# Second expert search: weight remainders on GpSimd, two of three gathered rows on VectorE, four dense U tiles behind the search

## The chip, the cores and the metric

The kernel runs on one core of one Trainium2 chip. The metric is the device time of one execution in microseconds (us). The core has a matrix engine (TensorE, PE in the profile; its weight loads are PEld), three elementwise engines (VectorE = DVE, ScalarE = ACT, GpSimd = POOL), and DMA queues that move data between HBM and the on-chip memory (SBUF). GpSimd also issues the indirect DMAs that gather rows by index. PSUM is the memory into which TensorE accumulates.

## The reference

One decoder block on 512 tokens of width 1024: three token mixers (forgetting attention, sliding window, memory attention) with gates, and then a product-key expert layer, which is what the change touches:

```python
def peer_ffn(h, w_q, keys1, keys2, u, v):
    q = (h @ w_q).astype(jnp.float32).reshape(B, S, PEER_HEADS, 2, half)
    s1 = jnp.einsum('bshd,hkd->bshk', q[..., 0, :], keys1)
    s2 = jnp.einsum('bshd,hkd->bshk', q[..., 1, :], keys2)
    v1, i1 = lax.top_k(s1, PEER_TOPK)
    v2, i2 = lax.top_k(s2, PEER_TOPK)
    cand = (v1[..., :, None] + v2[..., None, :]).reshape(B, S, PEER_HEADS, PEER_TOPK * PEER_TOPK)
    sv, si = lax.top_k(cand, PEER_TOPK)
    ...
    experts = e1 * N_KEYS + e2
    gates = jax.nn.softmax(sv, axis=-1)
    ...
        a = jnp.einsum('cd,ced->ce', h_c, u[e_c])
        act = jax.nn.gelu(a, approximate=False) * g_c
        return jnp.einsum('ce,ced->cd', act, v[e_c])
```

There are 8 heads, 128 keys in each half, 16 x 8 = 128 chosen experts for a token, and 16384 experts, each with one row of 1024 in `u` and one in `v`.

## The kernel before

**Tiles.** The tokens are four blocks of 128. Block 0 goes through the mixers first, blocks 1 to 3 together behind it. In the expert layer blocks 0 and 1 gather their rows: for each of the 128 choices one indirect DMA brings the `u` row or the `v` row of all 128 tokens (128 x 1024 floats), and one job multiplies and sums it. That makes 512 jobs in a fixed order (`JOBS`): the `u` rows of block 0, its `v` rows, then the same of block 1. Blocks 2 and 3 (`DENSE`) use no gathers: TensorE multiplies them with all of `u` and `v`, in 128 tiles of 128 experts each.

**A job** is one call of `step`. It first issues gathers, so that four rows (later six) lie ahead, into five row buffers, and then takes the oldest row. A `v` row of block 0 can be added in three ways: before PSUM is free, VectorE adds row times weight to `x1[0]` in SBUF (L890); with `apart`, ScalarE scales the row (L886) and GpSimd adds it to `x1[0]` (L887); otherwise VectorE adds row times weight to the tile `two` in PSUM (L893 for the first, L896 for the others), and `x1` gets `two` at the end of the block.

**Split weights.** For more exact products a weight is split into a rounded upper part `whi` (ScalarE, L119) and the remainder `wlo`. `load` fetches the weight, and first calls `pump`, which adds to the shared `credit[0]`, draws on a list of side work, and sets the credit to zero when that list is empty. `rest` makes the remainder: it adds `share[0]` to a counter, and each time the counter reaches one GpSimd does the subtraction (L129), else VectorE (L131). `mm3` then multiplies three times: upper by upper, lower by upper, upper by lower (L145 to L147). `gemm_tr` does this for one block of 128 output columns, 24 matmuls. The pool holds three `wlo` buffers.

**The stages in question.** The second search finds the experts of blocks 1 to 3. For each head two weight blocks (`w_pq`) go through `gemm_tr`, the result is multiplied with the keys (L754), and VectorE takes the best 16 of 128 for three blocks and two halves (`top16`, L711 to L715), then GpSimd sums the candidate pairs (L722) and VectorE takes the best 16 of 64, one head later. Two heads of scores are made ahead. `search` yields a cost of 1.6 for each top 16 of 128 and of 1.2 for each top 16 of 64, 105.6 in all. The loop around it spends these costs: for every `PER_ROW` of credit one job of block 0 is done, and at 104 / `FIRST_U` units each one dense U tile is computed (`dense_u`: 8 matmuls on unsplit data, then a Gelu on ScalarE, L1029 and L1031). The first 13 U tiles are fetched in this loop too. The first 183 jobs were done before, beside the mixers.

Behind the search comes the cover: `COVER` further dense U tiles on TensorE, while VectorE weighs the scores (`weigh`), derives the expert numbers of blocks 1 to 3 (`choose`, `numbers_of`, L806 to L850), and does jobs of block 0 between these parts. It starts U tile k with `FIRST_U` and ends with `KEPT` = `FIRST_U + COVER` = 32 tiles. `turn_block` then transposes the choices of a block (L1075, copied by ScalarE at L1077), and the spread begins: 64 batches in which VectorE builds one-hot sides (L1088), ScalarE scales them (L1091), TensorE multiplies them (L1103), while 25 further U tiles run, and 0.95 jobs a batch, every fourth of them apart. The last stage runs over all 128 tiles of `v`, with the remaining U tiles and jobs spread over it.

**Order.** Up to the end of the search a planner orders the instructions of each engine by estimated times and by rank; jobs have the lowest rank (`tc.high_priority(-LATER)`). From the cover on the order of TensorE, VectorE and GpSimd is that of the program.

Of the kernel before, what the change touches and what calls it, by code (L numbers as in the profile page):

```python
# [26 lines left out]
DENSE = (2, 3)  # L27
ND = len(DENSE)
TD = 128 * ND
FIRST_U, COVER, DURING, AFTER = 8, 24, 25, 0  # L30
PRE_U = 13
KEPT = FIRST_U + COVER
SPILT = (128 - KEPT) // 3
# [17 lines left out]
UNREAD = 36  # L51
LATER = 400
PACE = {"search": 20.0, "choose": 8.0, "rows": 3.5}
EARLY_ROWS, PER_ROW = 183, 4.6


@with_exitstack
def tile_block(ctx: ExitStack, tc: tile.TileContext, t: dict, out: bass.AP):
# [39 lines left out]
    due, share = [0.0], [0.0]  # L98
# [115 lines left out]
    def factors(sums, nb):  # L214

        ss = small_f(BIG, "rss", 2)[:, :nb]
        V.reduce_sum(ss, sums[:, :nb], axis=AX.X)
        return rsqrt_mean(ss, nb, D)

    def diagonals(r, nb):  # L220
        dg = small.tile([128, BIG, 128], F32, tag="dg", name="dg", bufs=1)
        for b in range(nb):
            A.activation(dg[:, b], ident, AF.Copy, scale=r[:, b:b + 1])
        return dg

    def turn(xs, g, hi, lo, dg=None, tags=("tp", "sc")):

        w = 128 * len(xs)
        for dc in range(KC):
            ps = bank(tags[dc % len(tags)])  # L230
            for b, x in enumerate(xs):
                dst, src = ps[:, b * 128:(b + 1) * 128], x[:, dc * 128:(dc + 1) * 128]
                if dg is None:
                    PE.transpose(dst, src, ident)
                else:
                    PE.matmul(dst, src, dg[:, b], start=True, stop=True)
            A.activation(hi[dc], ps[:, :w], AF.Copy, scale=g[:, dc:dc + 1])
            if lo:
                V.scalar_tensor_tensor(lo[dc], ps[:, :w], g[:, dc:dc + 1], hi[dc].bitcast(F32),
                                       op0=OP.mult, op1=OP.subtract)  # L240
# [614 lines left out]
    known, issued, done, ahead, flying, rpool = [2 * NJ], [0], [0], [AHEAD], {}, []  # L855
    begun_v = set()

    def step(apart=False):

        while issued[0] < min(known[0], done[0] + ahead[0] + 1):  # L860
            n = issued[0]
            issued[0] += 1
            b, tab, j = JOBS[n]
            if ahead[0] > AHEAD and n % (ROWS_IN + MORE) >= ROWS_IN:
                r = wp.tile([128, WSLOT], F32, tag="raw", name="row")[:, :D]
            else:
                r = rpool[0].tile([128, D], F32, tag="row", name="row", bufs=ROWS_IN)
            G.indirect_dma_start(out=r, out_offset=None, in_=t["peer_" + tab],  # L868
                                 in_offset=bass.IndirectOffsetOnAxis(ap=eidx[b][:, j:j + 1], axis=0))
            flying[n] = r  # L870
        n = done[0]
        done[0] += 1
        b, tab, j = JOBS[n]
        r, c = flying.pop(n), slice(j, j + 1)
        if tab == "u" and b and j == 0:
            A.copy(two[0], h2n[b])
        if tab == "u" and apart:
            G.tensor_tensor(r, r, h2n[b], op=OP.mult)
            A.activation(r, r, AF.Copy, accum_out=acts[b][:, c])
        elif tab == "u":  # L880
            scr = big.tile([128, D], BF16, tag="junk", name="scr")
            tc.keep_in_program_order(
                V.scalar_tensor_tensor(scr, r, 1.0, two[0] if b else h2n[b], op0=OP.mult, op1=OP.mult,  # L883
                                       accum_out=acts[b][:, c]))
        elif apart:
            tc.keep_in_program_order(A.activation(r, r, AF.Copy, scale=acts[b][:, c]))  # L886
            G.tensor_tensor(x1[b], x1[b], r, op=OP.add)  # L887
        elif not two:
            tc.keep_in_program_order(
                V.scalar_tensor_tensor(x1[b], r, acts[b][:, c], x1[b], op0=OP.mult, op1=OP.add))  # L890
        elif b not in begun_v:
            begun_v.add(b)
            tc.keep_in_program_order(V.tensor_scalar(two[0], r, acts[b][:, c], None, op0=OP.mult))  # L893
        else:
            tc.keep_in_program_order(
                V.scalar_tensor_tensor(two[0], r, acts[b][:, c], two[0], op0=OP.mult, op1=OP.add))  # L896
        if j == NJ - 1:
            if tab == "u":
                A.activation(acts[b], acts[b], AF.Gelu)
                V.tensor_mul(acts[b], acts[b], gate[b])  # L900
            else:
                V.tensor_add(x1[b], x1[b], two[0])
# [95 lines left out]
    def fetch_u_to(k):  # L998
        while u_next[0] <= min(k, NK - 1):
            fetch_u(u_next[0])  # L1000
            u_next[0] += 1
# [4 lines left out]
    def dense_u(k):  # L1006

        if k >= FIRST_U:
            fetch_u_to(min(max(k, PRE_U) + URING - 1, LAG) if k < LAG else k)
        w = u_raw.pop(k)  # L1010
        if split_u(k):
            if k % 2:
                hi, lo = (gp[0].tile([128, D], F32R, tag=tag, name=tag, bufs=1) for tag in ("uhi", "ulo"))
            else:
                hi, lo = halves_u[0][:, 0], halves_u[0][:, 1]
            A.copy(hi, w)
            yield
            V.tensor_sub(lo, w, hi.bitcast(F32))
            yield
            ps, hi, lo = bank("mm"), *(x.rearrange("p (n w) -> p n w", n=KC) for x in (hi, lo))  # L1020
            for dc in range(KC):
                mm3(ps[:, :TD], (hi[:, dc], lo[:, dc]), [x[dc] for x in h2s], dc == 0, dc == KC - 1)
            A.activation(ga(k), ps[:, :TD], AF.Gelu)
            return
        w = w.rearrange("p (n w) -> p n w", n=KC)
        yield
        ps = bank("mm")
        for dc in range(KC):
            PE.matmul(ps[:, :TD], w[:, dc], h2f[dc], start=dc == 0, stop=dc == KC - 1)  # L1029
            yield  # L1030
        A.activation(ga(k), ps[:, :TD], AF.Gelu)  # L1031
# [2 lines left out]
    h2T = [chunks(x) for x in pair(BIG)]  # L1034
    h2f = chunks(dp.tile([128, KC, TD], F32, tag="h2f", name="h2f", bufs=1))
    halves_u = []
    k_u, share[0] = 0, 0.0
    with tc.tile_pool(name="qb", bufs=2) as qq:
        turn([x1[b] for b in GROUPS[1]], g2, *h2T)
        spent, dg, credit[0] = 0.0, None, 0.0  # L1040
        for cost in search(qq, h2T, f, BIG):
            spent += cost
            if dg is None and spent > 12.0:
                V.tensor_copy(rstd[:, 1:NB], factors(sums, BIG))
                dg = diagonals(rstd[:, 2:NB], ND)
                turn([x1[b] for b in DENSE], g2, h2f, None, dg)
            while u_next[0] < PRE_U and spent > 6.0 * u_next[0]:
                fetch_u_to(u_next[0])
            credit[0] += cost
            while credit[0] >= PER_ROW and NJ <= done[0] < known[0]:  # L1050
                credit[0] -= PER_ROW
                with tc.high_priority(-LATER):
                    step(apart=True)
            if k_u < FIRST_U and spent > 104.0 / FIRST_U * (k_u + 1):
                list(dense_u(k_u))
                k_u += 1
    assert k_u == FIRST_U, (k_u, spent)

    cp = build.enter_context(tc.tile_pool(name="cp", bufs=1))
    ctx.enter_context(tc.manual_schedule(engines={mybir.EngineType.Pool, mybir.EngineType.DVE, mybir.EngineType.PE}))  # L1060
# [295 lines left out]
```

## Time and profile before

| | |
|---|---|
| median of 3 runs | 1589.84 us (lowest 1589.75; one run at 5559.83) |
| profiled execution | 1593.83 us, its span 1592.1 us |
| PE, PEld busy | 1514.5 us (95%), 1374.6 us (86%) |
| DVE, ACT, POOL busy | 1433.5 us (90%), 829.5 us (52%), 779.0 us (49%) |
| moved by DMA | 531.90 MB, mean 334 GB/s |
| VectorE remainders, L131 (128x1024) | 244 from the weight buffers, 304.2 us |
| rows added on GpSimd, L887 | 23, mean 2375 ns |

Times are counted from the start of the span. A row of a group names line, engine, operation, output and inputs, the shape, how often, the busy time with the mean of one, and the idle time of the engine just before it with what ended most of that. The search lies at about 640 to 755 us, the cover at 755 to 852, the spread from there to 1010, and the last stage goes to the end. A number of the form `(x572)` counts instructions.

### The profile page before, as it was taken

The numbers are of one execution on the slowest core, as the hardware profiler recorded it, in microseconds if no ns is written. First come the engines' busy times: TensorE is split into PE (matmuls) and PEld (weight loads), VectorE is DVE, ScalarE is ACT, GpSimd is POOL, SyncE is SP. The second block draws the span as 40 slices with busy tenths as digits, with TensorE's granted clock in tenths as the row PEclk, the third lists the DMA queues.
The fourth block names the chain that finished last, engine by engine and source line by source line (L and its number), as shares of the span: only waits on it lengthen the run. The fifth ranks groups of instructions, "written<-read, shape, count | busy, mean of one in ns | idle before, by whom it ended". The sixth has DMA issues, their size and how long they took to land.

```text
span 1592.1 us, 27209 instructions
## 1 busy us (share of the span) xinstructions
PE 1514.5 (95%) x9458; PEld 1374.6 (86%) x9458; DVE 1433.5 (90%) x2666; ACT 829.5 (52%) x1840; POOL 779.0 (49%) x639
## 2 busy tenths in 40 slices
PE   8999899999999989999995999899999999999998
PEld 7989799997888988999885898788888888888887
DVE  6678477989899999999899999799999999999998
ACT  7778336646345534454215998554454444454443
POOL 1100015768576455467744665455555454555451
PEclk9999999999999999999997999999999999999999
DMA  8677657898899899965897999999999999999995
GB/s 328 222 236 249 242 182 247 316 357 299 314 346 322 273 348 346 382 217 185 290 411 247 380 393 392 344 399 390 409 410 410 409 411 409 395 409 411 410 409 213
DMA packets 178361, 531.90 MB, mean 334 GB/s; under 512 B 17456, under 2 KB 46384, under 8 KB 178224
## 3 DMA queue, kind: packets, MB, share of 16 engines
q0 software_dynamic: 73728, 268.47, 44.8%
q1 hardware_dynamic: 94416, 225.95, 38.9%
q10 hardware_dynamic: 10080, 35.75, 5.6%
q8 instruction: 74, 1.21, 0.3%
q14 instruction: 63, 0.52, 0.1%
HBM read 515.42 MB, written 14.68 MB: 333 GB/s over the span
## 4 chain that ended last, share of the span: by engine, by line
PE 54%; DVE 13%; issue 12%; DMA 11%; POOL 6%; ACT 4%; DVEq 0%; POOLq 0%; SPq 0%; ACTq 0%
PE mm L146 8%; PE mm L1029 8%; PE mm L147 8%; PE mm L145 8%; DMA row<-in_peer_v_dram,eidx 5%; POOL row L868 4%; DMA row<-in_peer_u_dram,eidx 4%; DVE wlo L131 3%; PE sc L1103 3%; DVE two L896 2%; PE sc L146 1%; PE sc L147 1%; PE sc L145 1%; PE tp L145 1%; PE tp L146 1%
## 5 line engine op out<-in xcount | busy, mean ns | idle before, releaser
L868 POOL DMA_INDIRECT row<-in_peer_v_dram,eidx x256 | 320.9, 1254 | 287.1 <-DVE two L896 162.8
L868 POOL DMA_INDIRECT row<-in_peer_u_dram,eidx x256 | 318.2, 1243 | 237.2 <-DVE scr L883 135.0
L131 DVE TENSOR_TENSOR wlo<-raw,whi 128x1024 fp32r<-128x1024 f32 (+1 forms) x244 | 304.2, 1248 | 33.6 <-ACT whi L119 26.5
L896 DVE SCALAR_TENSOR_TENSOR two<-row,acts,two 128x1024 f32<-128x1024 f32 x176 | 226.2, 1285 | 3.4 <-DMA row<-in_peer_v_dram,eidx 1.1
L119 ACT CAST whi<-raw 128x1024 fp32r<-128x1024 f32 x146 | 152.6, 1050 | 100.4 <-PE mm L146 62.4
L883 DVE SCALAR_TENSOR_TENSOR scr<-row,own 128x1024 bf16<-128x1024 f32 x128 | 156.3, 1221 | 22.2 <-DMA row<-in_peer_u_dram,eidx 21.2
L883 DVE SCALAR_TENSOR_TENSOR scr<-row,two 128x1024 bf16<-128x1024 f32 x117 | 142.2, 1216 | 6.0 <-DMA row<-in_peer_u_dram,eidx 5.0
L203 POOL TENSOR_TENSOR rsy<-rsv,mhalf 128x4 f32<-128x4 f32 (+5 forms) x25 | 39.9, 1600 | 184.3 <-DVE rsv L202 130.5
L1156 ACT CAST ah<-ga 128x256 fp32r<-128x256 f32 x116 | 47.1, 407 | 156.3 <-PE tp L146 118.4
L145 PE MATMUL mm<-hhi,whi 128*128 128x384 f32 x320 | 110.1, 344 | 1.2 <-DVE mg L673 0.7
L1158 ACT CAST whi<-raw 128x1024 fp32r<-128x1024 f32 x96 | 100.4, 1048 | 18.2 <-DMA raw<-in_peer_v_dram 12.7
L146 PE MATMUL mm<-hlo,whi 128*128 128x384 f32 x320 | 109.7, 343 | 0.0
L147 PE MATMUL mm<-hhi,wlo 128*128 128x384 f32 x320 | 108.9, 340 | 0.0
L146 PE MATMUL sc<-wlo,ah 128*128 128x512 f32 x256 | 101.4, 396 | 6.3 <-DVE wlo L131 6.3
L145 PE MATMUL mm<-whi,hhi 128*128 128x256 f32 (+1 forms) x360 | 103.7, 290 | 2.9 <-DVE g L604 1.9
L146 PE MATMUL mm<-wlo,hhi 128*128 128x256 f32 (+1 forms) x360 | 102.6, 286 | 1.7 <-DVE wlo L131 1.6
L147 PE MATMUL mm<-whi,hlo 128*128 128x256 f32 (+1 forms) x360 | 101.9, 285 | 0.8 <-DVE hlo L662 0.8
L147 PE MATMUL sc<-whi,al 128*128 128x512 f32 x256 | 101.8, 398 | 0.0
L145 PE MATMUL sc<-whi,ah 128*128 128x512 f32 x256 | 101.3, 396 | 0.2 <-ACT whi L1158 0.2
L145 PE MATMUL tp<-whi,ah 128*128 128x512 f32 x256 | 101.1, 395 | 0.0
L146 PE MATMUL tp<-wlo,ah 128*128 128x512 f32 x256 | 100.8, 394 | 0.0
L147 PE MATMUL tp<-whi,al 128*128 128x512 f32 x256 | 100.7, 393 | 0.0
(322 smaller groups left out, 4544.9 us busy)
## 6 DMA issues: line engine op xcount, KB each, us to landing
raw<-in_peer_v_dram SPq DMA_DIRECT2D x96, 512.0 KB
hhi<-in_uT_dram ACTq DMA_DIRECT2D x68, 512.0 KB
raw<-in_w_tr_dram SPq DMA_DIRECT2D x48, 512.0 KB
raw<-in_w_nat_dram SPq DMA_DIRECT2D x40, 512.0 KB
last<-in_peer_v_dram SPq DMA_DIRECT2D x32, 512.0 KB
hhi<-in_uT_dram SPq DMA_DIRECT2D x26, 512.0 KB
raw<-in_w_o_dram SPq DMA_DIRECT2D x24, 512.0 KB
gd<-st SPq DMA_DIRECT2D x24, 512.0 KB
```

Of the source, the lines that this page charges most:

```text
L119: (cast or A.copy)(hi[:, :n * w], raw[:, :n * w])
L131: V.tensor_sub(lo, raw, hi.bitcast(F32))
L145: PE.matmul(ps, lh, rh, start=first, stop=False)
L146: PE.matmul(ps, lh, rl, start=False, stop=False)
L147: PE.matmul(ps, ll, rh, start=False, stop=last)
L868: G.indirect_dma_start(out=r, out_offset=None, in_=t["peer_" + tab], in_offset=bass.IndirectOffsetOnAxis(ap=eidx[b][:, j:j + 1], axis=0))
L883: V.scalar_tensor_tensor(scr, r, 1.0, two[0] if b else h2n[b], op0=OP.mult, op1=OP.mult, accum_out=acts[b][:, c]))
L896: V.scalar_tensor_tensor(two[0], r, acts[b][:, c], two[0], op0=OP.mult, op1=OP.add))
L1029: PE.matmul(ps[:, :TD], w[:, dc], h2f[dc], start=dc == 0, stop=dc == KC - 1)
L1103: PE.matmul(ps[:, u], o[:, 1, u], o[:, 0, u], start=True, stop=True)
L1156: A.copy(ah, a)
L1158: A.copy(hi, raw)
```

## The change

Three constants and three lines of the second search are changed. While the search runs, `share[0]` is 1.0 in place of 0.0, so that all 16 remainders of the query weights go to GpSimd. A job counts 4.2 in place of 4.6, and it is done apart (ScalarE and GpSimd) only if its number is divisible by three and the cost spent is under 94; the others go to VectorE and `two`. Four U tiles run in the search in place of eight, and 28 in place of 24 in the cover.

```diff
-FIRST_U, COVER, DURING, AFTER = 8, 24, 25, 0
+FIRST_U, COVER, DURING, AFTER = 4, 28, 25, 0
...
-EARLY_ROWS, PER_ROW = 183, 4.6
+EARLY_ROWS, PER_ROW, APART, NO_APART = 183, 4.2, 3, 94.0
...
-    k_u, share[0] = 0, 0.0
+    k_u, share[0] = 0, 1.0
     with tc.tile_pool(name="qb", bufs=2) as qq:
         turn([x1[b] for b in GROUPS[1]], g2, *h2T)
         spent, dg, credit[0] = 0.0, None, 0.0
...
             while credit[0] >= PER_ROW and NJ <= done[0] < known[0]:
                 credit[0] -= PER_ROW
                 with tc.high_priority(-LATER):
-                    step(apart=True)
+                    step(apart=done[0] % APART == 0 and spent < NO_APART)
             if k_u < FIRST_U and spent > 104.0 / FIRST_U * (k_u + 1):
                 list(dense_u(k_u))
                 k_u += 1
     assert k_u == FIRST_U, (k_u, spent)
+    share[0] = 0.0
```

`KEPT`, and with it the split between gates kept on chip and gates sent through HBM, stays at 32, and `LAG` at 57.

## The prediction

> **What bounds the kernel now.** I read the page's span in slices, then a table of busy time over six stretches cut where the work changes: second search, dense U tiles behind it ("cover"), a gap, the ramp of the spread, the spread, the last stage.
>
> ```profile
> 655.00:755.00 100.00, 99.48 (x572) 95.00 (x572) 98.29 (x585) 48.13 (x73) 61.42 (x63) 1.00 0.67 240
> 755.00:835.00 80.00, 79.21 (x369) 69.41 (x367) 74.63 (x110) 14.19 (x30) 50.75 (x42) 1.00 0.92 350
> 835.00:852.00 17.00, 0.26 (x3) 0.02 (x1) 16.65 (x23) 0.83 (x2) 8.63 (x9) 0.59 0.90 321
> 852.00:870.00 18.00, 16.00 (x88) 14.67 (x89) 17.46 (x21) 15.52 (x57) 5.57 (x6) 0.82 0.49 165
> 870.00:1010.00 140.00, 136.93 (x849) 125.08 (x848) 126.63 (x193) 124.23 (x458) 85.18 (x69) 0.99 1.03 376
> 1010.00:1592.00 582.00, 562.54 (x3215) 490.34 (x3213) 558.96 (x660) 268.74 (x394) 282.37 (x209) 0.99 0.99 392
> ```
>
> The columns are the stretch, its length, the busy us of PE, weight load, DVE, ACT and POOL, the granted clock, DMA share and GB/s. In the search PE (99.5 of 100 us) and DVE (98.3) are both full, DMA is not (0.67). In the cover both stay full. From 835 to 852 PE does 0.26 us and DVE 16.65 of 17: DVE alone decides when the spread starts. The spread is full on PE and DMA, the last stage on DMA (0.99), with DVE at 96%.
>
> The chain in order of time and the waits say how the cover ends:
>
> ```profile
> 762.15 72.79 PE mm L1029 x336
> 834.93 0.33 PE tp L1075 x3
> 835.26 18.74 issue
> ```
>
> ```profile
> ACT eT L1077 <- DVE own L850: 14.9, 1, 14.9
> ```
>
> PE has multiplied its last cover tile and turned block 0 by 835.3; then 18.7 us pass in which only DVE works, and ACT's copy of the turned block waits 14.9 us for DVE's last job before the spread.
>
> ```profile
> L1088 DVE TENSOR_TENSOR o<-tp,eT x64: 1212/1215/1222, 852.2 to 997.4; 128x1024 f32<-128x1024 f32 x64
> ```
>
> L1088 is the spread's first work on DVE. So its start, 852.2, is the later of DVE's end (852) and PE's end (835). What the change takes from DVE pays for 17 us, then PE decides.
>
> **How many rows move.** `pump` sets the shared credit to zero at each weight load, as its work list is empty by then. So rows are counted per head: 9.6 units for head 0, 13.2 each for heads 1 to 4, then 43.2 without a load. At 4.6 a row this gives 2, 4 x 2 and 9: 19 rows. At 4.2 it gives 2, 4 x 3 and 10: 24 rows. Of these, numbers 183 to 206, the condition (divisible by 3, cost under 94) holds for seven; 17 go to DVE. The 19 agree with the trace:
>
> ```profile
> L887 POOL TENSOR_TENSOR mg<-mg,row x23: 2353/2367/2420, 676.4 to 895.2; 128x1024 f32<-128x1024 f32 x23
> ```
>
> 19 of the 23 are the search's, 4 stand in the spread. The cover keeps 36 rows, the spread 60, so the last stage gets 209 rows instead of 214.
>
> **DVE, part by part.** Rows by groups and by line in 640 to 755, and one collision from the timeline:
>
> ```profile
> L131 DVE TENSOR_TENSOR wlo<-raw,whi x14: 1197/1224/3709, 639.3 to 726.0; 128x1024 fp32r<-128x1024 f32 x14
> L131 DVE TENSOR_TENSOR wlo<-raw,whi 128x1024 fp32r<-128x1024 f32 x14 | 23.6, 1683 | 0.5 <-ACT whi L119 0.5
> 715.88 2.41 POOL L887 TENSOR_TENSOR mg<-mg,row 128x1024 f32<-128x1024 f32 x1
> 715.68 3.71 DVE L131 TENSOR_TENSOR wlo<-raw,whi 128x1024 fp32r<-128x1024 f32 x1
> L896 DVE SCALAR_TENSOR_TENSOR two<-row,acts,two x176: 1275/1284/1291, 773.3 to 1573.1; 128x1024 f32<-128x1024 f32 x176
> L711 DVE MAX8 best<-cand 128x8 f32<-128x64 f32 x24 | 4.3, 210 | 1.6 <-POOL cand L722 1.6
> ```
>
> Removed: 16 lower parts, 14 of them in this window with 23.6 us and two ahead of it at 1.22: 26.0 us. Undisturbed the 14 would be 17.1 us, so 6.5 us of it are collisions like the one shown, where 1.22 became 3.71 beside a GpSimd addition. Added: 17 rows into PSUM at 1.284, 21.8 us; that group stays within 1275 to 1291 ns over 176 calls although GpSimd adds beside some of them, so I give it no stretch. Gone also: 1.6 us in which DVE waits for the last candidates behind GpSimd's additions.
>
> GpSimd's additions now run on into the cover and disturb DVE there:
>
> ```profile
> L887 POOL TENSOR_TENSOR mg<-mg,row 128x1024 f32<-128x1024 f32 x6 | 14.2, 2365 | 0.1
> L835 DVE TENSOR_TENSOR hot<-hot 128x1024 bf16<-128x1024 bf16 x6 | 6.1, 1013 | 0.0
> L819 DVE TENSOR_TENSOR rj<-rj,p 128x128 f32<-128x128 f32 x3 | 3.7, 1223 | 0.1
> L820 DVE TENSOR_TENSOR rj<-p,rj 128x128 f32<-128x128 f32 x3 | 0.9, 291 | 0.1
> L807 DVE TENSOR_SCALAR p<-sh 128x128 f32<-128x128 uint32 x3 | 3.3, 1113 | 0.1
> L806 DVE TENSOR_SCALAR sh<-pos 128x128 uint32<-128x128 uint32 x3 | 0.7, 220 | 0.0
> L791 DVE TENSOR_TENSOR gate<-ex,gden 128x128 f32<-128x128 f32 x3 | 2.8, 1034 | 0.0
> ```
>
> Against their equals (L820, L806) the excess is 2.8 us for L819, 2.6 for L807 and about 1.8 for each of L791 and L835: 9.0 us. With seven additions instead of 19, and none behind cost 94, it goes. Sum for DVE: -26.0 + 21.8 - 1.6 - 9.0 = **-14.8 us**; it ends the cover at 837.5.
>
> **PE.** Four tiles move; each is 3.45 us, by ACT's Gelu that follows each:
>
> ```profile
> 772.81 0.38 ACT L1031 ACTIVATE ga<-mm 128x256 f32<-128x256 f32 x1 [3.07 <-PE mm L1029]
> 776.26 0.38 ACT L1031 ACTIVATE ga<-mm 128x256 f32<-128x256 f32 x1 [3.07 <-PE mm L1029]
> 655.41 0.34 PE L145 MATMUL mm<-hhi,whi 128*128 128x384 f32 x1
> 659.09 0.34 PE L145 MATMUL mm<-hhi,whi 128*128 128x384 f32 x1
> ```
>
> So 13.8 us leave the search and come back in the cover; nothing vanishes. PE was full in both, hence its end stays at 835 plus whatever it now waits for. The pair of matmuls, seven triples apart, gives 0.526 us a triple, 4.2 us for the 24 matmuls of one weight block. GpSimd must deliver one lower part per block at 2.37 (L887, the same shape) instead of DVE's 1.22. Its load in the window:
>
> ```profile
> L887 POOL TENSOR_TENSOR mg<-mg,row 128x1024 f32<-128x1024 f32 x14 | 33.4, 2384 | 4.9 <-ACT row L886 4.7
> L868 POOL DMA_INDIRECT row<-in_peer_v_dram,eidx x23 | 24.8, 1077 | 12.5 <-DVE rss L217 3.5 <-POOL cand L722 2.9 <-DVE mg L890 1.5
> L722 POOL TENSOR_TENSOR cand<-v 128x48 f32<-128x48 f32 (+2 forms) x32 | 13.0, 418 | 28.1 <-DVE v L714 18.4 <-DVE v L711 8.9 <-DMA raw<-in_w_pq_dram 0.7
> ```
>
> After: 16 x 2.37 + 7 x 2.37 + 28 x 1.08 + 13.0 = 98 us of 115, where it was 71. The queue is in order: behind an addition that waits for ACT's scaling, a row issue that waits for a free row buffer, or a candidate sum that waits for DVE (27.3 us of waits now), a lower part now stands still, and PE behind it. PE works up to two heads ahead of DVE, and three `wlo` buffers are filled ahead, so most is hidden; the opening, where PE runs block after block at 4.2 us against 2.37 + 1.08 and gaps, is not. GpSimd's subtraction is not in the trace: PE's loss lies between 0 and 18.4 (16 x 1.15, every extra microsecond felt) before waits; nearest to the 4.2 us period I take 4. PE ends at 839; with about 2 us for the order of the two I put the start of the spread at 841, **11 us earlier**. ScalarE loses 12 scalings and nothing waits for it.
>
> The Trainium skill, "GPSIMD Engine Reference", section "Engine selection", speaks against the move: two-input elementwise work belongs on VectorE, GpSimd being about two times slower. The trace agrees (2.37 to 1.22); felt in full it would be the 18.4 us, and the rule leaves out that DVE is the engine that ends last here.
>
> **The last stage.** One full stretch of it, and DVE's waits for rows from 870 on:
>
> ```profile
> 1400.00:1500.00 100.00, 99.23 (x583) 87.47 (x582) 99.43 (x102) 48.39 (x71) 50.68 (x38) 1.00 1.03 410
> L896 DVE SCALAR_TENSOR_TENSOR two<-row,acts,two 128x1024 f32<-128x1024 f32 x137 | 176.2, 1286 | 3.0 <-DMA row<-in_peer_v_dram,eidx 1.1
> L883 DVE SCALAR_TENSOR_TENSOR scr<-row,two 128x1024 bf16<-128x1024 f32 x117 | 142.2, 1216 | 6.0 <-DMA row<-in_peer_u_dram,eidx 5.0
> ```
>
> Five rows fewer are 5 x 0.524 MB (128 x 1024 x 4 bytes) = 2.6 MB; at 410 GB/s, or the 392 of the whole stage, 6.4 to 6.7 us; on DVE 5 x 1.28 = 6.4. PE's matmuls stay. Bounds 0 and 6.7; I take **5**, as DMA and DVE are both near full.
>
> **Given back.** From 835 to 870 DMA is below its ceiling only because PE and DVE stand; with the gap gone fewer tiles and rows lie ready when the spread, at share 1.03, begins. The slack is 17 x 0.10 + 18 x 0.51 = 11 us, of which 0 to 5 may return; I take **2**.
>
> Sum: -11 - 5 + 2 = **-14**. The profiled execution took 1593.83 us (span 1592.1), so 1579.8 there; on the median of 1589.84, which is 4 lower, **1576**.
>
> **Rivals.**
> - *DMA decides from the cover on.* For: share 0.92, 1.03, 0.99 behind 755. Against: DVE waited for rows only 6.1 us from 870 to the end. Then only the five rows count: 1589.84 - 6 = 1584. Chance 0.17.
> - *GpSimd's queue starves PE (slower).* Place: lower parts behind candidate sums and row issues. Price: 18.4 us plus half of the 27.3 us of waits, 32 us; PE ends at 867, the spread starts 15 later, less 5: 1600. It decides once PE loses over 17 us, and the sign turns at 22. Against: two heads of lead. Chance 0.13.
> - *New collisions at the opening.* Ten old rows still add SBUF to SBUF there:
>
> ```profile
> L890 DVE SCALAR_TENSOR_TENSOR mg<-row,acts,mg 128x1024 f32<-128x1024 f32 x10 | 12.8, 1280 | 0.0
> ```
>
> Four or five lower parts on GpSimd meet them, each good for up to the 2.5 us that L131 lost at 715.7: 10 us, DVE ends at 848, 4 gained instead of 11: 1583. Chance 0.08. The Trainium skill, "SBUF — State Buffer", section "Who interferes with whom", says as much: a DVE instruction with two SBUF inputs contends with a GpSimd one that reads SBUF, one with a single SBUF input does not. The collision at 715.7 and the unmoved L896 agree.
> - *It doesn't do what it says.* The planner gives rows the lowest rank and may put the 17 behind the last head; DVE would then wait on gathers (4.3 us from issue to scaling in the chain below) once or twice: 1585. Chance 0.07.
>
> ```profile
> 749.09 4.34 DMA row<-in_peer_v_dram,eidx
> ```
>
> The forecast keeps 0.55; alone its range is 1567 to 1582 (DVE's 837.5 with the full 6.5, to PE losing 10). With the rivals at 1583 to 1585 and the nearer part of the slower one, 1565 to 1597 holds eight in ten. A measurement here tells about 2%, 32 us, from no change; faster by that needs 1558, slower 1622, and no case reaches either: 0.03, 0.93, 0.04.
>
> **What would show it.** Right: 16 `wlo` on POOL near 2.37 us; L896 from the 660s at 1.28; no three-microsecond L791, L807, L819; the gap behind the last cover tile under 5 us; the spread's first L1088 near 841; last stage about 5 us shorter. Wrong: PE waiting on `wlo` for over 10 us, DVE waiting on row DMAs in the search, or a spread that lasts longer.

## The result, and the profile after

The changed kernel takes 1583.97 us (median of 10 runs, 1579.78 to 1587.23), the kernel before 1591.55 (median of 10 runs, one of them at 5559.83): ratio 0.9946, 95% interval 0.9929 to 0.9963, some 8.6 us (5.9 to 11.3). The profiled execution of it took 1584.12 us, its span 1582.3.

Executions of one program differ by several us in parts that the change doesn't touch, so I measure from marks in the program. The last L673, an addition of VectorE to `mg`, stands ahead of the second search, L781 is its first instruction behind the search, and the one-hot build (L1088, L1089 after) opens the spread. First the marks of the kernel before, then of the kernel after, from the view of a line (duration least/median/greatest in ns, first and last start in us):

```profile
L673 DVE TENSOR_TENSOR mg<-g,mm x16: 409/418/423, 174.1 to 635.7; 128x256 f32<-128x256 f32 x16
L781 DVE TENSOR_TENSOR ex<-best x2: 292/607/922, 228.7 to 755.7; 128x128 f32<-128x128 f32 x1, 128x384 f32<-128x384 f32 x1
```

```profile
L673 DVE TENSOR_TENSOR mg<-g,mm x16: 408/414/423, 174.3 to 633.1; 128x256 f32<-128x256 f32 x16
L781 DVE TENSOR_TENSOR ex<-best x2: 293/422/551, 228.2 to 758.8; 128x128 f32<-128x128 f32 x1, 128x384 f32<-128x384 f32 x1
L1089 DVE TENSOR_TENSOR o<-tp,eT x64: 1208/1215/1218, 847.6 to 991.4; 128x1024 f32<-128x1024 f32 x64
```

From L673 to L781, the search, 120.0 us became 125.7; from L781 to the spread, the cover, 96.5 became 88.8. Together, 216.5 became 214.5: the stage at which the change aims gained 2.0 us, not 11. From the last build to the end 594.7 became 590.9, 3.8 us less with five rows fewer. The spread (145.2 to 143.8) and the 2.6 us by which the last L673 came earlier make up the rest of the 9.8 us between the two spans. The 2.6 us are no gain of the change: the seventh last L673, ahead of the first remainder on GpSimd, came 3.6 us earlier already (614.84 for 618.45), in code that is the same. From there to the last L673 the changed kernel lost 1.0 us, 18.2 for 17.3, although two remainders had left VectorE in that stretch; a pair of L890 rows in it took 4.06 us, where a pair took 2.60 before.

Where the search lost, by the groups of VectorE from 640 to 760 and two collisions from the timeline, kernel after:

```profile
L896 DVE SCALAR_TENSOR_TENSOR two<-row,acts,two 128x1024 f32<-128x1024 f32 x16 | 20.3, 1271 | 0.0
L890 DVE SCALAR_TENSOR_TENSOR mg<-row,acts,mg 128x1024 f32<-128x1024 f32 x9 | 19.0, 2115 | 0.0
```

```profile
653.40 2.43 POOL L129 TENSOR_TENSOR wlo<-raw,whi 128x1024 fp32r<-128x1024 f32 x1
653.60 3.32 DVE L890 SCALAR_TENSOR_TENSOR mg<-row,acts,mg 128x1024 f32<-128x1024 f32 x1
657.78 2.42 POOL L129 TENSOR_TENSOR wlo<-raw,whi 128x1024 fp32r<-128x1024 f32 x1
657.43 3.85 DVE L890 SCALAR_TENSOR_TENSOR mg<-row,acts,mg 128x1024 f32<-128x1024 f32 x1
```

The new rows into PSUM (L896) take 1.27 us, undisturbed. The old rows in SBUF (L890), 1.28 us each before, take 2.12 on average: five of the ten behind the last L673 meet a remainder on GpSimd, take 2.17 to 3.85 us, and end 1.08 to 1.10 us behind the remainder's end. Four of the five start behind the remainder, one 0.35 us ahead of it.

Where the cover gained, and where it gave some back (groups of VectorE there, then ScalarE's timeline, kernel after):

```profile
L819 DVE TENSOR_TENSOR rj<-rj,p 128x128 f32<-128x128 f32 x3 | 1.0, 317 | 0.1
L791 DVE TENSOR_TENSOR gate<-ex,gden 128x128 f32<-128x128 f32 x3 | 0.9, 391 | 0.0
L807 DVE TENSOR_SCALAR p<-sh 128x128 f32<-128x128 uint32 x3 | 0.7, 245 | 0.1
L788 DVE TENSOR_REDUCE gden<-ex 128x24 f32<-128x384 f32 x1 | 0.6, 553 | 5.6 <-ACT ex L784 5.6
```

```profile
759.53 1.28 ACT L784 ACT_TABLE_LOAD   x1 [6.83 <-DVE ex L781]
760.83 0.40 ACT L784 ACTIVATE ex<-ex,rstd 128x128 f32<-128x128 f32 x1
761.25 1.28 ACT L1031 ACT_TABLE_LOAD   x1
762.54 0.38 ACT L1031 ACTIVATE ga<-mm 128x256 f32<-128x256 f32 x1
762.94 1.28 ACT L784 ACT_TABLE_LOAD   x1
764.24 0.69 ACT L784 ACTIVATE ex<-ex,rstd 128x128 f32<-128x128 f32 x2
```

The three-microsecond instructions of the cover are gone. But ScalarE now puts a tile's Gelu between the first Exp and the other two, which costs two table loads of 1.28 us, and VectorE waits 5.6 us for the Exp.

TensorE, by the chain in order of time of the kernel after, and its last transpose from the timeline:

```profile
762.98 81.38 PE mm L1029 x368
844.69 4.66 issue
```

```profile
844.41 0.27 PE L1076 MATMUL tp<-cst,gate 128*128 128x128 f32 x1
```

It ends the cover at 844.4 where it ended at 835; the gap behind it shrank from 18.7 us to 4.7. VectorE's 847.6 still sets the start of the spread, by 2 us over TensorE and the copy.

### The profile page after: what moved, and what is told of

Its sections match the earlier page's. It is cut to its first block, busy times and chain, and to the rows that moved or that the text cites. A ratio compares the mean times of both kernels' runs of the same rounds, so it can differ in the third digit from the quotient of the medians.

```text
span 1582.3 us, 27174 instructions
## 1 busy us (share of the span) xinstructions
PE 1512.7 (96%) x9458; PEld 1373.8 (87%) x9458; DVE 1422.0 (90%) x2661; ACT 819.9 (52%) x1831; POOL 789.2 (50%) x643
## 4 chain that ended last, share of the span: by engine, by line
PE 58%; DVE 14%; issue 10%; DMA 10%; POOL 5%; ACT 2%; POOLq 0%; SPq 0%; DVEq 0%; ACTq 0%
PE mm L1029 9%; PE mm L146 9%; PE mm L145 9%; PE mm L147 9%; DMA row<-in_peer_v_dram,eidx 6%; POOL row L868 5%; PE sc L1104 3%; DVE two L896 2%; DVE wlo L131 2%; DMA row<-in_peer_u_dram,eidx 2%; PE sc L147 2%; PE sc L146 2%; PE tp L145 2%; PE tp L146 2%; PE sc L145 2%
## 5 line engine op out<-in xcount | busy, mean ns | idle before, releaser
L868 POOL DMA_INDIRECT row<-in_peer_v_dram,eidx x256 | 328.9, 1285 | 289.2 <-DVE two L896 164.1
L131 DVE TENSOR_TENSOR wlo<-raw,whi 128x1024 fp32r<-128x1024 f32 (+1 forms) x228 | 278.1, 1221 | 34.2 <-ACT whi L119 30.0
L896 DVE SCALAR_TENSOR_TENSOR two<-row,acts,two 128x1024 f32<-128x1024 f32 x189 | 242.5, 1283 | 4.1 <-DMA row<-in_peer_v_dram,eidx 1.9
```

Of the source, the lines that this page charges most:

```text
L131: V.tensor_sub(lo, raw, hi.bitcast(F32))
```

## The experiments

All are compared by the same marks, each row from one profiled execution; the ratios come from 6 to 12 runs, beside runs of the kernel before. "Stage" is search and cover together. "PE end" is the start of the last transpose of block 0, counted from the last L673. "Last build to end" goes from the start of the last one-hot build to the end of the span.

| kernel | search | cover | stage | PE end | last build to end | ratio to before (95%) |
|---|---|---|---|---|---|---|
| before | 120.0 | 96.5 | 216.5 | 199.3 | 594.7 | 1 |
| changed | 125.7 | 88.8 | 214.5 | 211.3 | 590.9 | 0.9946 (0.9929 to 0.9963) |
| e1, remainders alone | 120.0 | 96.6 | 216.6 | 199.4 | 593.5 | 0.9991 (0.9977 to 1.0006) |
| e2, rows alone | 132.9 | 85.6 | 218.5 | 205.5 | 590.3 | 0.9991 (0.9974 to 1.0008) |
| e3, tiles alone | 120.0 | 99.3 | 219.3 | 210.0 | 591.8 | 1.0018 (0.9995 to 1.0040) |
| e4, changed without the tiles | 125.9 | 85.6 | 211.5 | 205.1 | 590.0 | 0.9939 (0.9917 to 0.9961) |
| e5, six remainders on VectorE | 122.6 | 85.6 | 208.2 | 205.0 | 589.8 | 0.9937 (0.9917 to 0.9957) |
| e6, changed with 19 rows | 121.1 | 88.2 | 209.3 | 208.4 | 591.7 | 0.9949 (0.9931 to 0.9968) |
| e7, e5 without the tiles | 122.9 | 85.6 | 208.5 | 200.5 | 587.1 | 0.9928 (0.9908 to 0.9947) |
| e8, weighing first | 125.8 | 87.5 | 213.3 | 212.5 | 587.2 | 0.9962 (0.9948 to 0.9975) |
| e9, e7 with every second row apart | 125.3 | 85.6 | 210.9 | 205.6 | 587.4 | 0.9910 (0.9889 to 0.9932) |
| changed, again | 125.8 | 88.7 | 214.5 | 212.0 | 586.7 | 0.9946 (0.9926 to 0.9967) |

### One part at a time

**e1, the remainders alone**: `k_u, share[0] = 0, 1.0` ahead of the search and `share[0] = 0.0` behind it, all else as before.

> Only the remainders move to GpSimd; 19 rows stay on ScalarE and GpSimd, eight tiles stay in the search. Stage length is counted from the last L673 to the first L1088 of the spread: 216.5 us in the kernel before, 214.5 in the changed one. Theory (VectorE's sum sets the stage, minus what GpSimd's tensor work takes from its two-SBUF-input instructions): 26 us of remainders go, but 16 x 2.37 + 19 x 2.37 + issues is over 120 us of GpSimd work in 115, so its additions run further into the cover and disturb VectorE there by more than the 9 us of before, and about 10 us are lost at the opening; stage about 205 to 212, last stage unchanged. Rival (GpSimd's queue starves TensorE): remainders stand behind 19 additions, TensorE loses over 20 us, stage 225 or more, total slower by 8 us or more.

Stage 216.6, nothing gained: neither my 205 to 212 nor the rival's 225. Groups of VectorE in the search of e1:

```profile
L890 DVE SCALAR_TENSOR_TENSOR mg<-row,acts,mg 128x1024 f32<-128x1024 f32 x10 | 21.5, 2152 | 0.0
L711 DVE MAX8 v<-s 128x8 f32<-128x128 f32 x48 | 11.1, 279 | 5.7 <-ACT s L757 5.7
L711 DVE MAX8 best<-cand 128x8 f32<-128x64 f32 x24 | 4.1, 215 | 9.8 <-POOL cand L722 9.8
```

The remainders' time comes back as 8.7 us of collisions (21.5 for 12.8), 9.8 us of waiting for candidate sums that stand behind GpSimd's work (1.6 before), and 5.7 us for scores, whose cause was not followed. The cover, where I expected more disturbance, stays at 96.6. TensorE's multiplications wait 1.0 us for remainders (waits of e1):

```profile
PE mm L147 <- POOL wlo L129: 1.0, 1, 1.0
```

So the queue does cost, but at the candidates and not where the rival put it.

**e2, the rows alone**:

```diff
-EARLY_ROWS, PER_ROW = 183, 4.6
+EARLY_ROWS, PER_ROW, APART, NO_APART = 183, 4.2, 3, 94.0
-                    step(apart=True)
+                    step(apart=done[0] % APART == 0 and spent < NO_APART)
```

> Only the rows move: 24 jobs in the search, 17 of them on VectorE; remainders stay on VectorE. Theory: VectorE +21.8 for the rows, -1.6 for the last candidates, -9 for the cover's collisions, -3 to -4 for fewer collisions with remainders: stage 216.5 + 7 to 8 = 224; the last stage is 5 us shorter with its five rows less; total +2 us. Rival (only DMA decides behind the search): the stage's 7 us do not show at the end, total -6 us.

Stage 218.5 where 224 was expected: the cover gained 10.9 us, not 9 (1.4 of it as the wait for the Exp is 2.5 us, 3.9 before), and the remainders lost their collisions nearly whole (VectorE's group in the search of e2):

```profile
L131 DVE TENSOR_TENSOR wlo<-raw,whi 128x1024 fp32r<-128x1024 f32 x13 | 17.4, 1337 | 0.5 <-ACT whi L119 0.5
```

Rows and remainders need each other: alone each comes out even, together (e4) they gain 5 us of stage.

**e3, the tiles alone**: `FIRST_U, COVER` from 8, 24 to 4, 28.

> Only the four dense U tiles move behind the search. Theory: VectorE sets the start of the spread in the kernel before (TensorE has 17 us to spare), so the stage stays at 216.5 within 1 us and the total within 2 us; the gap behind TensorE's last cover tile stays near 17 us or shrinks by what TensorE then idles in the search. Rival (TensorE bounds the search): the search gets up to 13.8 us shorter for VectorE too, stage near 205.

The search did not get shorter by a tenth, so TensorE did not bound it: its time there was filled with tiles, and without four of them it was busy for 110.2 of the 120.0 us where it had been for 116.6. Its end came 10.7 us later. The stage got 2.8 us longer, which I had not expected; six GpSimd additions start in the cover where five did, and L812 met one of them, 3.6 us in all for 0.9 (L812's group in the cover, before and e3):

```profile
L812 DVE SCALAR_TENSOR_TENSOR ri<-p,p 128x128 f32<-128x128 f32 x3 | 0.9, 292 | 0.1
```

```profile
L812 DVE SCALAR_TENSOR_TENSOR ri<-p,p 128x128 f32<-128x128 f32 x3 | 3.6, 1197 | 0.1
```

**e4, the changed kernel without the tiles**: `FIRST_U, COVER` back to 8, 24.

> The changed kernel with eight tiles in the search again. Theory: VectorE's end is not touched, stage 214.5 within 2 us; TensorE fills with tiles the time in which it waits for remainders, so its last cover tile ends some us earlier relative to the last L673 than in the changed kernel (211). Rival (the tiles in the search stand between weight blocks and delay the scores): stage 4 to 14 us longer, total slower by as much.

Stage 211.5, 3 us shorter. TensorE ended 6 us earlier, as expected, but the 3 us are VectorE's: the wait for the Exp is 2.5 us here, 5.6 in the changed kernel.

```profile
DVE gden L788 <- ACT ex L784: 2.5, 1, 2.5
```

### The two losses

**e8, the Exp together**: `UNWEIGHED` from 14 to 0, which puts the weighing ahead of the cover's tiles in the program.

> The changed kernel with the weighing ahead of the cover's tiles in the program (UNWEIGHED 0 for 14); TensorE's and VectorE's instructions are the same, ScalarE runs the three Exp together, where the changed kernel has a Gelu with two table loads between the first and the other two. Theory (moving the tiles cost 3 us by that): VectorE's wait for the Exp falls from 5.6 to 2.5 us, stage 214.5 to about 211.5 to 212.5, where TensorE's end (211.2) takes over. Rival (the tiles cost by TensorE's later end): the wait falls but the stage stays at 214.

The wait is 2.5 us, but the stage gained only 1.2: VectorE now waits 1.8 us for the turned block (VectorE's waits in the cover of e8). With four more tiles in the cover, TensorE's end is the next bound.

```profile
DVE gden L788 <- ACT ex L784: 2.5, 1, 2.5
DVE o L1089 <- ACT eT L1078: 1.8, 1, 1.8
```

**e5, the first six remainders on VectorE**, the ones that met L890:

```diff
-    k_u, share[0] = 0, 1.0
+    k_u, share[0] = 0, 0.0
...
             spent += cost
+            share[0] = 1.0
```

> The changed kernel, but the first six of the 16 remainders stay on VectorE (share 1.0 only from the first yield of the search); these six stood among the last additions of L890, two SBUF inputs each, whose mean rose from 1.28 to 2.12 us in the changed kernel. Theory (collisions at the opening): L890 is back at 1.28 us, VectorE loses 6 x 1.22 = 7.3 and regains about 10 us; from the last L673 to the end of the search 125.7 becomes about 123, the stage 214.5 becomes about 211.5; total 2 to 3 us faster than the changed kernel. Rival (GpSimd's lateness and not the port is what hurts: VectorE waits for rows that GpSimd issues late): L890 stays long or DMA waits appear, stage 214 or more.

The search took 122.6 us, 3.1 less. The collisions with these rows fell by 6.2 us, from 8.7 to 2.5, and four of the six remainders, those behind the last L673, cost VectorE 4.9; some 2 us came from shorter waits (2.7 to 0.5). L890 did not come back to 1.28 in full (VectorE's group in the search of e5):

```profile
L890 DVE SCALAR_TENSOR_TENSOR mg<-row,acts,mg 128x1024 f32<-128x1024 f32 x10 | 15.3, 1532 | 0.0
```

GpSimd's first remainder now starts at 656.1, and the one row that still meets it takes 3.87 us. Another 3.2 us came in the cover, as here the Exp happen to stand together; so this run changes two things, and only what L890 does speaks of the collisions.

**e7, both**: e5 with `FIRST_U, COVER` = 8, 24.

> The changed kernel with both edits: first six remainders on VectorE, and eight tiles in the search, 24 behind it. Theory: the effects add, as they sit in different places (opening; Exp of the weighing): stage 211.5 with the tiles back, less 3: 208.5; total about 6 us faster than the changed kernel and 14 faster than the kernel before. Rival (TensorE's end bounds the stage as soon as VectorE is quicker): TensorE's last cover tile 205 after the last L673, then the copy, so the start is at 206.5 at the earliest and the gain is cut if TensorE ends later than that.

Stage 208.5 as expected, but e5 had it already: with the Exp together, where the four tiles stand makes no difference to VectorE (122.9 and 85.6 against 122.6 and 85.6), only to TensorE's end, 200.5 against 205.0.

### Rows

**e6, the changed kernel with 19 rows**: `PER_ROW` 4.6.

> The changed kernel with 4.6 units for a row as before: 19 rows in the search, 13 or 14 of them on VectorE, 214 in the last stage. Theory: stage 4 to 5 us shorter (210), from the last L1089 to the end about 3 us longer (594 against 591); total about 1 to 2 us faster than the changed kernel, within the noise. Rival (rows in the search are free, as VectorE fills waiting time with them): stage stays at 214.5, total 3 us slower.

The search is 4.6 us shorter and the wait for the Exp 3.1, but the stage only 5.2: VectorE waits for the turned block at its end (waits of e6), so here too TensorE is the next bound.

```profile
DVE o L1089 <- ACT eT L1078: 2.5, 1, 2.5
```

The total is the same (0.9949 against 0.9946). What a row in the search costs VectorE there it saves in the last stage: over all runs that stage is 588.7 us with 209 rows (eight runs, 586.7 to 590.9) and 592.9 with 214 (four, 591.7 to 594.7), 4.2 us for five rows. Kernels that were measured side by side give 3.8 (before and changed), 2.5 (e1 and e3 against e2 and e4) and 3.7 (e6 against e5, e7 and e8). The changed kernel alone differs by 4.2 between its two profiles, so the size is rough.

**e9, every second row apart**: e7 with `APART` 2.

> The kernel of the late share and the eight tiles, with every second row of the search on ScalarE and GpSimd in place of every third: 10 or 11 of the 24 rows there, 13 or 14 on VectorE. Theory (VectorE sets the stage, GpSimd has room as six remainders have left it, and rows into PSUM are not disturbed): VectorE loses 3 or 4 rows of 1.28 us in the search: stage 208.5 becomes about 204, if TensorE ends by then (it ended 200.5 after the last L673). Rival (GpSimd's queue is full: its additions delay candidates and remainders): VectorE waits for candidates, stage 208 or longer.

The profiled execution went against the theory: stage 210.9. VectorE waits for gathered rows (its group in the search of e9), and for candidates only 0.3 us, so the rival's reason is not it either. That GpSimd, with three additions more in its queue, issues these rows too late fits, but is not shown.

```profile
L896 DVE SCALAR_TENSOR_TENSOR two<-row,acts,two 128x1024 f32<-128x1024 f32 x13 | 16.6, 1276 | 4.6 <-DMA row<-in_peer_v_dram,eidx 4.6
```

Its timed runs have the lowest ratio of all, 0.9910, but it ran on another chip than e7 and the intervals overlap; whether e9 beats e7 stays open.

**The changed kernel again.**

> The changed kernel itself, once more, beside the kernel of the late share on the same chip: ratio to the kernel before 0.993 to 0.996, stage 214.5 within 1 us, the wait for the Exp 5.6 us, L890 at 2.1 us. If stage and ratio differ by more, the differences of 2 to 3 us between the earlier runs are noise.

214.5 and 5.6 us once more, though L673 came at 639.3 in place of 633.1. Search, cover and stage hold to 0.1 us here, while the start of the search moved by 6.2, the last stage by 4.2 and TensorE's end by 0.7.

## Why the prediction came near, and where its steps failed

The forecast was 1576 with 14 us gained, in a range of 1565 to 1597; measured are 1584 and 8.6. The direction, the bound (VectorE sets the start of the spread) and the last stage held. The middle of the sum did not: the spread was to start 11 us earlier, and the stage gained 2.0. So the nearness is in part luck. The range is wide enough to hold the kernel before as well, and by the marks the change is worth about 6 us (2.0 and 4.2); what the timed runs show beyond that, inside their interval, is not explained.

- **Rows moved: right.** GpSimd makes 10 additions in all, 7 of them in the search, and 16 remainders at 2.40 us where 2.37 was taken.
- **The last stage, 5 us: right in size,** 4.2 over all runs. Nothing is seen of the 2 us given back to DMA: the spread is not longer than before in any run but e9. The rival in which only DMA decides and five rows fewer are worth 6 us forecast 1584, which is what was measured, but by coincidence: e6 has all 214 rows in its last stage and still takes 0.9949 (0.9931 to 0.9968) of the time before, and e2 has five rows fewer and takes 0.9991, its lower bound 0.9974 above the 0.996 of that rival.
- **VectorE, -14.8 us: the term of the search was mis-sized.** -5.8 was summed for it, +5.7 measured. 8.7 of the 11.5 us between are the L890 rows behind the last L673, five of which take 2.17 to 3.85 us in place of 1.28. I had that as a rival, with four or five meetings, a price of 10 us, 1583 as its time and a chance of 0.08; the sum itself has nothing for it. The kernel before shows where they would meet: its L131 at 639.35, 649.37, 651.70 and 658.63 stand among its L890 rows from 636.04 to 661.01. A further 2.4 us of the -26.0 could not show in the search, as two of the 16 remainders stand ahead of the last L673 in the kernel before. The cover's -9.0 was right: -7.7 was measured, and 1.7 us of waiting for the Exp stand against it (5.6, 3.9 before), so 9.4 went.
- **"PE was full in both, hence its end stays at 835": failed.** It ended 12.0 us later after L673, and e3 shows 10.7 by the tiles alone. The other delay is not the remainders, for which 4 us were taken: e1 moves TensorE's end by 0.1, e2, with the rows alone, by 6.2, and e4, with both, by 5.8. How the rows delay it stays open. A busy share of 99% did not mean a bound, as TensorE had work to fill with. In the changed kernel that did not cost the stage, as VectorE still ended last; e8 and e6 show that it does as soon as VectorE is 2 us quicker.
- **An edit taken at nothing: the Exp.** In the changed kernel a tile's Gelu falls between the first Exp and the other two, and VectorE waits 5.6 us, 3.1 more than in e4 and e8. The four moved tiles do not do it by themselves: in e3, e5 and e6 they are moved too, and the three Exp stand together. What makes the planner of ScalarE's order choose so was not tested.
- **The rival on the other side, GpSimd's queue, did not decide.** Waits of matmuls for remainders exist (4.5 us, the view of waits of the kernel after from 640 to 760), but TensorE had that to spare:

```profile
PE mm L147 <- POOL wlo L129: 4.5, 2, 3.5
```

In e1 the same queue, with twelve additions more, takes the whole gain.

By the Trainium skill, "SBUF — State Buffer", section "Who interferes with whom", the L890 rows had to meet the remainders and the rows into PSUM had not; both agree with 2.12 and 1.27 us. For instructions with one SBUF input the Trainium skill's rule holds only outside what it calls the 2-port perf modes, a condition that the prediction left out. The prediction's rows show a case that its short form misses: L807, with one SBUF input, took 1.11 us on average where L806 took 0.22. Whether L807 runs in such a mode, no run here shows.

e7 and e9 beat the kernel before by more than the changed kernel does (0.9928 and 0.9910 to 0.9946), with overlapping intervals; by the marks e7's stage is 6 us shorter.

## What to carry to other kernels

When work goes to GpSimd, list which VectorE instructions with two SBUF inputs run in exactly those microseconds, lowest-ranked leftovers too; the collision can cost more than the move saves. Here, adding into PSUM kept VectorE out of that: L896 took 1.265 to 1.292 us in all 189 calls of the changed kernel. And an engine that is 99% busy in a stage is its bound only if the stage gets shorter when its work is taken out, so ask what of that work is filler.

## What the runs showed of the hardware

A VectorE instruction with two SBUF inputs that by its record starts 0.35 us ahead of a GpSimd subtraction (657.43 and 657.78) still ends 1.1 us behind it, with 3.85 us for 1.28. With a longer lead it goes the other way (timeline of the kernel after):

```profile
624.35 1.28 DVE L890 SCALAR_TENSOR_TENSOR mg<-row,acts,mg 128x1024 f32<-128x1024 f32 x1
625.06 2.83 POOL L129 TENSOR_TENSOR wlo<-raw,whi 128x1024 fp32r<-128x1024 f32 x1
```

Here VectorE starts 0.71 us ahead and takes its 1.28 us, and the subtraction takes 2.83 for 2.40. The timelines of the other runs agree: leads of 0.70 to 0.72 us win in five more of them, and the longest lead that loses is 0.55 us (e3, 702.61 and 703.16, 4.05 us for 1.22). So one of the two waits for the other, and which one is not simply read from the starts of the records.

Small instructions suffer as much in absolute terms: in e3 one L812 of 0.29 us took 3.01. And two activation tables in turn on ScalarE cost 1.28 us a change, which sat on VectorE's path here.
